# Layer A's projections as seven block products (Strassen) in a streaming encoder step

## The chip, the core and the metric

One core of a Trainium2 chip runs the whole kernel in one launch. The metric is the device time of that launch in microseconds, the median of several runs; the kernel before takes 2946.37 us (three runs, 2944.8 to 2947.03).

## What is computed

One inference step of a trunk with one layer of each kind (float32 everywhere). 640 token rows, 512 of a new stream and 8 x 16 of running ones, are 2048 wide. Layer A, the part that changes:

```python
h = rmsnorm(x, norm_a)                        # 640 x 2048
z = h @ w_in_a                                # 2048 -> 2 * 4096
u, gate = z[..., :4096], z[..., 4096:]
# 4 groups of 1024 channels; trailing mean over 2, 4, 8, 16 rows minus the row itself
y[group] = (mean(u[group], window) - u[group]) @ w_grp_a[group]     # 1024 -> 1024
x = x + (y * scale * silu(gate)) @ w_out_a    # 4096 -> 2048
```

The last 15 rows of u of every stream are outputs too. Then come one shared projection to keys and values, layer B (attention with a forgetting term over the keys of past and new rows, a gate, an output projection) and a final norm.

## The kernel before

Channels lie on the 128 partitions and the 640 tokens along the free dimension, in two halves of 320 (`HALF`). To multiply in float32r with nearly float32's accuracy, each operand is split in two: `hi` is the float32r copy (ScalarE), `lo` what is left (VectorE, `split`). A product is then three matmuls, hi·hi, hi·lo and lo·hi: `mm3` issues them for both halves, six matmuls of 320 columns for each block of 128 x 128 weights (line 93).

`gemm_pair` makes two output blocks of 128 channels: it loads weights in chunks of 2 x 128 rows by 256 columns (`wchunk`, four raw buffers, three of each split part) and accumulates over the contraction in PSUM. `u_pair` makes two blocks of u, takes the pooling differences (on VectorE, lines 333 to 360) and keeps them split; `gate_pair` makes two blocks of the gate; `y_pair` multiplies the differences of a group of 1024 channels by the group's map and the gate; `out_pairs` multiplies two such pairs (512 channels) by the rows of the output projection and adds the result to the residual `acc` in SBUF (line 413). The order is by group: four u pairs, then gates and maps by turns, with the output projection after every second map pair.

The start of layer A runs inside the first u pair: x comes in eighths of 256 channels, is turned by TensorE and split block by block while the first pair's matmuls already use the earlier blocks. The row norm is not applied to x but to the results (`R`, a factor per token).

TensorE's instructions stand in the order in which they are written (`manual_schedule`); the other engines' are ordered by a planner with a cost model. Small side work is given to TensorE's stream by generators (`work`, `tick`). All DMAs are issued on SP's queue. At the end of layer A, `after` splits the new stream, ScalarE squares it and GpSimd sums the squares (lines 466 to 473); the keys' projection (`proj`, tile `mmb`) follows at once.

## Time and profile before

| | |
|---|---|
| median of three runs | 2946.37 us |
| span of the profiled execution, first to last instruction | 2944.0 us |
| layer A, up to the first matmul of the next projection | 1610.6 us |
| TensorE busy | 2921.5 us, 99% |
| VectorE busy | 1457.7 us, 50% |
| ScalarE busy | 847.9 us, 29% |
| GpSimd busy | 34.7 us, 1% |
| moved by DMA | 293 MB, mean 100 GB/s |

The three runs are timed without a profile; the profiled execution is known by its span. A matmul's busy time overlaps that of its neighbours, so 99% says that TensorE always has one under way, not that it runs at its peak.

### The profile page before, as it was taken

What the parts mean: (1) busy time and instruction counts of PE and PEld (TensorE: products, weight loads), DVE (VectorE), ACT (ScalarE), POOL (GpSimd) and SP (SyncE); (2) the same over time, 40 slices, a digit from 0 to 9 for tenths busy, and PEclk for the clock granted to TensorE, in tenths of its full rate; (3) what the DMA queues carried; (4) which work ended last, traced back from release to release, by engine and by line L of the source; (5) the groups of instructions that cost most, each with busy time, mean ns of one, the idle gap of its engine ahead of it and who ended that gap; (6) DMA issues with size and microseconds to landing.
All of it is one profiled execution on the core that took longest, in us unless ns stands there. A gap on an engine that the chain in (4) does not pass through costs nothing.

```text
span 2944.0 us, 47606 instructions
## 1 busy us (share of the span) xinstructions
PE 2921.5 (99%) x19573; PEld 2828.4 (96%) x19573; DVE 1457.7 (50%) x2587; ACT 847.9 (29%) x1560; POOL 34.7 (1%) x73
## 2 busy tenths in 40 slices
PE   9999999999999999999999999999999999999998
PEld 9999999999999999999999899999999999999786
DVE  6423344333445333554337755655656666556434
ACT  5222222221222212222224232333333333334222
POOL 0000000000000000000003000000000000000000
PEclk9999999999999999999999999999999999999999
DMA  4222222222222222222224655455554555554822
GB/s 149 81 78 76 76 79 78 81 75 76 79 77 83 75 76 76 79 80 78 76 76 140 132 122 119 112 119 123 134 119 114 119 120 121 118 119 108 145 86 108
DMA packets 610282, 293.04 MB, mean 100 GB/s; under 512 B 281024, under 2 KB 595712, under 8 KB 609936
## 3 DMA queue, kind: packets, MB, share of 16 engines
q1 hardware_dynamic: 610064, 290.00, 38.5%
q8 instruction: 153, 2.51, 0.4%
q14 instruction: 65, 0.53, 0.1%
HBM read 261.28 MB, written 28.64 MB: 98 GB/s over the span
## 4 chain that ended last, share of the span: by engine, by line
PE 93%; DMA 2%; DVE 2%; SPq 1%; ACT 1%; issue 1%; DVEq 0%; POOL 0%; POOLq 0%; ACTq 0%
PE mm L93 35%; PE mmb L93 29%; PE mmx L93 17%; PE mmf L900 4%; PE po L832 2%; PE tb L117 1%; PE f L900 1%; PE ss L733 1%; DMA xt<-xres 1%; SPq L938 1%; DVE yn L941 0%; DMA raw<-in_w_in_b 0%; PE sp L743 0%; PE op L845 0%; PE op L844 0%
## 5 line engine op out<-in xcount | busy, mean ns | idle before, releaser
L78 DVE TENSOR_TENSOR wlo<-raw,whi 128x512 fp32r<-128x512 f32 x480 | 337.6, 704 | 793.6 <-ACT whi L75 791.4
L75 ACT ACTIVATE whi<-raw 128x512 fp32r<-128x512 f32 x480 | 302.7, 631 | 1012.2 <-PE mm L93 588.8
L93 PE MATMUL mmb<-xh,whi 128*128 128x320 f32 x2048 | 483.1, 317 | 2.6 <-DVE acc L413 2.6
L93 PE MATMUL mmb<-xh,wlo 128*128 128x320 f32 x2048 | 467.1, 309 | 0.0
L93 PE MATMUL mmb<-xl,whi 128*128 128x320 f32 x2048 | 466.9, 309 | 0.0
L93 PEld LDWEIGHTS mmb<-xh,whi 128*128 128x128 f32 x2048 | 337.1, 189 | 8.9 <-issue 6.5
L93 PEld LDWEIGHTS mmb<-xh,wlo 128*128 128x128 f32 x2048 | 342.9, 188 | 0.0
L93 PEld LDWEIGHTS mmb<-xl,whi 128*128 128x128 f32 x2048 | 342.8, 188 | 0.0
L93 PE MATMUL mm<-xh,whi 128*128 128x320 f32 x1408 | 325.8, 313 | 1.3 <-ACT xh L258 1.3
L93 PE MATMUL mm<-xl,whi 128*128 128x320 f32 x1408 | 321.7, 310 | 0.3 <-DVE xl L259 0.2
L93 PE MATMUL mm<-xh,wlo 128*128 128x320 f32 x1408 | 321.3, 309 | 0.0
L142 DVE TENSOR_TENSOR wlo<-raw,whi 128x512 fp32r<-128x512 f32 x272 | 188.3, 693 | 204.5 <-ACT whi L140 200.4
L140 ACT ACTIVATE whi<-raw 128x512 fp32r<-128x512 f32 x272 | 171.6, 632 | 377.4 <-PE mmb L93 232.1
L93 PEld LDWEIGHTS mm<-xl,whi 128*128 128x128 f32 x1408 | 235.6, 188 | 1.4 <-DVE xl L259 1.3
L93 PEld LDWEIGHTS mm<-xh,wlo 128*128 128x128 f32 x1408 | 235.8, 188 | 0.0
L93 PEld LDWEIGHTS mm<-xh,whi 128*128 128x128 f32 x1408 | 234.0, 188 | 1.8 <-ACT xh L258 1.5
L131 DVE TENSOR_TENSOR raw<-raw,cols 128x512 f32<-128x512 f32 x256 | 169.3, 676 | 4.8 <-DMA raw<-in_w_kv 2.2
L93 PE MATMUL mm<-mh,whi 128*128 128x320 f32 x688 | 157.4, 310 | 0.4 <-ACT whi L75 0.4
L93 PE MATMUL mm<-mh,wlo 128*128 128x320 f32 x688 | 156.7, 309 | 0.0
L93 PE MATMUL mm<-ml,whi 128*128 128x320 f32 x688 | 156.4, 308 | 0.0
L93 PE MATMUL mmx<-xh,whi 128*128 128x320 f32 x640 | 147.2, 311 | 0.0
L93 PE MATMUL mmx<-xh,wlo 128*128 128x320 f32 x640 | 145.8, 309 | 0.0
(306 smaller groups left out, 4187.9 us busy)
## 6 DMA issues: line engine op xcount, KB each, us to landing
raw<-in_w_in_a SPq DMA_DIRECT2D x256, 256.0 KB, 2.7
raw<-in_w_out_a SPq DMA_DIRECT2D x128, 256.0 KB, 2.8
raw<-in_w_kv SPq DMA_DIRECT2D x128, 256.0 KB, 3.0
raw<-in_w_in_b SPq DMA_DIRECT2D x128, 256.0 KB, 3.0
raw<-in_w_grp_a SPq DMA_DIRECT2D x64, 256.0 KB, 2.7
kc<-in_cache_k SPq DMA_DIRECT2D x64, 256.0 KB, 4.8
vc<-in_cache_v SPq DMA_DIRECT2D x16, 1024.0 KB, 7.6
raw<-in_w_out_b SPq DMA_DIRECT2D x64, 256.0 KB, 3.0
```

Source lines behind the costliest of these rows:

```text
L75: a = nc.scalar.activation(hi, x, AF.Copy)
L78: nc.vector.tensor_tensor(lo, x, hi.bitcast(F32), op=ALU.subtract)
L93: nc.tensor.matmul(acc_[:, s, :HALF], w, x[:, s * HALF : (s + 1) * HALF], start=f, stop=l)
L117: nc.tensor.transpose(out, x, ident[:n, :n])
L131: nc.vector.tensor_tensor(r, r, raws[n][1].unsqueeze(2).to_broadcast([P, 4, P]), op=ALU.mult)
L140: nc.scalar.activation(hi, raw, AF.Copy)
L142: nc.vector.tensor_tensor(lo, raw, hi.bitcast(F32), op=ALU.subtract)
L733: nc.tensor.matmul(sp[rows, b % 2 * PAST : (b % 2 + 1) * PAST], qs[:, rows], kct[:, b * PAST : (b + 1) * PAST], start=True, stop=True)
L832: nc.tensor.matmul(po[32 * q : 32 * q + 32, :P], pts[:, j, 32 * q : 32 * q + 32], vc[:, 4 * q + j, :], start=(j == 0), stop=False)
L900: nc.tensor.matmul(out, (ol if q == 2 else oh)[:, k, ts], wl if q == 1 else wh, start=first and q == 0, stop=last and q == 2)
L938: dma(xt[at].rearrange("p t (j r) -> p t j r", r=32), xres[n * 512 : (n + 1) * 512].rearrange("(j c) (t a r) -> a c t j r", c=32, a=4, r=3 ...
```

## The change

*Seven products for eight.* The 640 tokens and the channels are cut in two: a pair of output blocks, a pair of contraction blocks and the two halves of tokens form 2 x 2 blocks. Instead of eight block products, seven products of sums and differences are made (Winograd's form). Of the weights, `prep` makes four sums per pair on VectorE and splits seven operands; of x, `blocks_b` and `blocks_t` make the same once per pair of contraction blocks (`Side`). `product` is one of the seven: three matmuls of 320 columns. `pair8` runs a pair of u or gate blocks: four slabs of 512 contraction rows, in each all seven products, each in its own PSUM bank (bank 7 is left for small transposes); `combine` makes the four result blocks out of the seven banks. The output projection does the same over 512 rows of a half group (`out_pair`): now all 1024 rows of a group in one accumulation. The maps of the groups (`y_pair`) stay plain.

*New order.* All u and gate pairs come first (32 units); the pooling differences and the gates go to DRAM and come back for the maps; then, group by group, four map pairs and eight output pairs.

*Start.* x is loaded by rows, normalised by rows (`norm_a` included), turned, and only then split into blocks and sums; `first_unit` runs the first pair with the products that need no sums of x ahead of the others. `R` is no longer needed in layer A.

*Moved between engines.* The sliding sums of the pooling go from VectorE to GpSimd (2 to 8 adds per u pair), as do half of the sums of x, and some weight sums of the last 16 chunks. Stores of layer A go from SP's queue to GpSimd's. The residual lies in DRAM (`xacc`): `out_pair` adds to it by accumulating DMAs on GpSimd's queue, one of 640 KB and two of 160 and 320 KB for each pair of output blocks; for the last group the sum is loaded back and finished on VectorE.

*Buffers.* PSUM is one tile of eight banks, given out by hand. SBUF pools are laid anew, with waits by tile where one takes over the place of another. In layers after A only the banks, the names of buffers and the place of x (DRAM, loaded back at the start of layer B) change.

```diff
+    OPER = {"m1": (0, 0), "m6": (5, 5), "m5": (4, 3), "m7": (3, 4), "m2": (2, 2), "m3": (6, 1), "m4": (1, 6)}
...
+    def blocks_b(sd, x4):
+        sd.bh, sd.bl = (bslot(sd.j, q, [P, 3, HALF], F32R) for q in "hl")
+        nc.scalar.activation(sd.bh, x4[:, 1:4, :], AF.Copy)
+        nc.vector.tensor_tensor(sd.bl, x4[:, 1:4, :], sd.bh.bitcast(F32), op=ALU.subtract)
...
+    def blocks_t(sd, x4, t, eng=None):
+        eng = eng or nc.vector
+        eng.tensor_tensor(t[:, 0, :], x4[:, 0, :], x4[:, 1, :], op=ALU.subtract)
+        eng.tensor_tensor(t[:, 1, :], x4[:, 2, :], x4[:, 0, :], op=ALU.add)
+        eng.tensor_tensor(t[:, 2, :], x4[:, 2, :], t[:, 0, :], op=ALU.add)
+        eng.tensor_tensor(t[:, 3, :], x4[:, 3, :], t[:, 2, :], op=ALU.subtract)
+        sd.th, sd.tl = (tslot(sd.j, q, [P, 4, HALF], F32R) for q in "hl")
+        nc.scalar.activation(sd.th, t, AF.Copy)
+        nc.vector.tensor_tensor(sd.tl, t, sd.th.bitcast(F32), op=ALU.subtract)
...
+    def prep():
+        n = nprep[0]
+        raw = loaded.pop(n).rearrange("p (a b) (s n) -> p a (b s) n", a=2, n=P)
+        if loads[n][0] == "s":
+            sums = wa.tile([P, 2, 4, P], F32, tag="sums", name="sums")
+            nc.vector.tensor_tensor(sums[:, :, 0:2, :], raw[:, :, 1:3, :], raw[:, :, 0:1, :].to_broadcast([P, 2, 2, P]),
+                                    op=ALU.subtract)
+            eng = nc.gpsimd if n >= len(loads) - 16 else nc.vector
+            eng.tensor_tensor(sums[:, :, 2, :], sums[:, :, 1, :], raw[:, :, 1, :], op=ALU.add)
+            eng.tensor_tensor(sums[:, :, 3, :], raw[:, :, 3, :], sums[:, :, 2, :], op=ALU.subtract)
+            two, (wh, wl) = wbufs(n, [P, 2, 7, P])
+            todo = [(raw, slice(1, 4), slice(0, 3)), (sums, slice(0, 4), slice(3, 7))]
+        else:
+            two, (wh, wl) = wbufs(n, [P, 2, 4, P])
+            todo = [(raw, slice(0, 4), slice(0, 4))]
+        for src, a, b in todo:
+            if two is not None:
+                split(two[0][:, :, b, :], two[1][:, :, b, :], src[:, :, a, :])
+            else:
...
+    def advance():
+        d = ndone[0]
+        ahead = 3 if d < NA else 4
+        while nprep[0] < min(d + ahead, len(loads)):
+            if nload[0] <= nprep[0]:
+                fetch()
+            prep()
+        while nload[0] < min(nprep[0] + 3, len(loads)):
+            fetch()
...
+    def product(bank, m, wts, kk, sd, first, last):
+        wh, wl = wts
+        a, b = OPER[m]
+        for q, (w, x) in enumerate(((wh, sd.hi(b)), (wh, sd.lo(b)), (wl, sd.hi(b)))):
+            nc.tensor.matmul(bank[:, :HALF], w[kk][:, a, :], x, start=first and q == 0, stop=last and q == 2)
...
+    def pair8(hook=None):
+        pp = {m: banks[:, j, :] for j, m in enumerate(ORDER)}
+        for s in range(4):
+            wts = parts.pop(0)
+            advance()
+            for j, m in enumerate(ORDER):
+                for kk in range(2):
+                    product(pp[m], m, wts, kk, xs_[2 * s + kk], s + kk == 0, s == 3 and kk == 1)
+                if j == 6:
+                    done()
+                if hook is not None:
+                    hook(s, j)
+                if j in (2, 5):
+                    tick()
+        return pp
...
+        v, u, e = cvue
+        nc.scalar.activation(v, pp["m1"][:, :HALF], AF.Copy)
+        nc.vector.tensor_tensor(u, v, pp["m6"][:, :HALF], op=ALU.add)
+        nc.vector.tensor_tensor(e, u, pp["m5"][:, :HALF], op=ALU.subtract)
+        put("c22", e, "m7", ALU.subtract)
+        nc.vector.tensor_tensor(u, u, pp["m7"][:, :HALF], op=ALU.subtract)
+        put("c11", v, "m2", ALU.add)
+        put("c12", e, "m3", ALU.add)
+        put("c21", u, "m4", ALU.add)
...
+    units = [("u", 0, 0)]
+    for n in range(1, 16):
+        units += [("u", n // 4, n % 4), ("g", (n - 1) // 4, (n - 1) % 4)]
+    units += [("g", 3, 3)]
...
+    half_rows(0)
+    for q in range(4):
+        dma(gains[q], i["norm_a"][0][q * 512 : (q + 1) * 512].partition_broadcast(P))
+    half_rows(1)
+    fetch()
+    half_rows(2)
+    half_rows(3)
+    half_rows(4)
+    for _ in range(2):
+        fetch()
+    ssq = small.tile([P, TT, 4], F32, name="ssq")
...
+            nc.scalar.activation(banks[:, 7, :], rows[t][q * 512 // n][:, c : c + 512], AF.Square, accum_out=ssq[:, t, q : q + 1])
...
+            nc.vector.scalar_tensor_tensor(r, r, rs, gains[q], op0=ALU.mult, op1=ALU.mult)
...
+    for j in range(8):
+        blocks_b(xs_[j], x4s[j])
+        if j in (1, 3, 5):
+            prep()
+            for _ in range({1: 1, 3: 0, 5: 3}[j]):
+                fetch()
+    for j in range(8):
+        t = tslot({1: 4, 3: 5, 5: 6}[j], "h", [P, 4, HALF]) if j in (1, 3, 5) else x4slot()
+        blocks_t(xs_[j], x4s[j], t, nc.gpsimd if j % 2 else None)
...
+    def first_unit():
+        pp = {m: banks[:, j, :] for j, m in enumerate(ORDER)}
+        held = [parts.pop(0) for _ in range(4)]
+        for ms in (("m1", "m2", "m3"), ("m6", "m5", "m7", "m4")):
+            for s in range(4):
+                for kk in range(2):
+                    for m in ms:
+                        product(pp[m], m, held[s], kk, xs_[2 * s + kk], s + kk == 0, s == 3 and kk == 1)
+                if ms[0] == "m6":
+                    done()
+                    if s > 1:
+                        prep()
+        return pp
...
-                    nc.vector.tensor_tensor(nx[:, e0:], cur[:, e0:], cur[:, e0 - sh : UW - sh], op=ALU.add)
...
+                nc.gpsimd.tensor_tensor(nx[:, e0:], cur[:, e0:], cur[:, e0 - sh : UW - sh], op=ALU.add)
...
+            store2(dscr[4 * g + p][b * P : (b + 1) * P, :], dd)
...
+    def gate_pair(g, p, hook=None):
+        pp = pair8(hook)
+        sg = x4slot()
+        combine(pp, lambda name: [(sg[:, WHERE[name], :], slice(0, HALF))])
+        for b in range(2):
+            v = sg[:, 2 * b : 2 * b + 2, :]
+            nc.scalar.activation(v, v, AF.Silu)
+        store2(pair_rows(gscr[4 * g + p]), sg.rearrange("p (k s) n -> p k (s n)", k=2))
...
+    def d_pair(g, j, dk):
+        raw = ps_.tile([P, 2, NT], F32, tag="sg", name="draw", bufs=2)
+        dma(raw, pair_rows(dscr[4 * g + j]))
+        dk.append([tslot(j, q, [P, 2, NT], F32R) for q in "hl"])
+        split(dk[-1][0], dk[-1][1], raw)
...
+        blocks_b(y_[p], m4)
+        blocks_t(y_[p], m4, x4slot())
...
-                    a = halves(acc[:, 2 * c + b, :])
-                    nc.vector.tensor_tensor(a, pp[b][:, :, :HALF], a, op=ALU.add)
...
+    def out_pair(g, c, x1=None):
+        pp = {m: bank()[:, :HALF] for m in ORDER}
+        wts = [parts.pop(0), parts.pop(0)]
+        advance()
+        def go(m, s):
+            for kk in range(2):
+                product(pp[m], m, wts[s], kk, y_[2 * s + kk], s + kk == 0, s + kk == 2)
+        for m, s in [(m, s) for s in range(2) for m in ORDER[:4]] if c == 0 else [(m, s) for m in ORDER[:4] for s in range(2)]:
+            go(m, s)
+        u = misc.tile([P, HALF], F32, tag="cu", name="cu")
+        o4 = m4slot() if c % 2 or x1 is not None else x4slot()
+        nc.scalar.activation(o4[:, 3, :], pp["m1"], AF.Copy)
+        nc.vector.tensor_tensor(u, o4[:, 3, :], pp["m6"], op=ALU.add)
+        nc.vector.tensor_tensor(o4[:, 2, :], u, pp["m5"], op=ALU.subtract)
+        nc.vector.tensor_tensor(o4[:, 0, :], o4[:, 2, :], pp["m7"], op=ALU.subtract)
+        nc.vector.tensor_tensor(o4[:, 1, :], u, pp["m7"], op=ALU.subtract)
+        nc.gpsimd.dma_start(pair_rows(xacc[c]), o4.rearrange("p (k s) n -> p k (s n)", k=2), accum_op=ALU.add)
+        if x1 is not None:
+            for k in range(2):
+                dma(x1[k], xacc[c][k * P : (k + 1) * P, :])
+        for m, s in (("m2", 0), ("m3", 0), ("m2", 1), ("m3", 1), ("m4", 0), ("m4", 1)):
+            go(m, s)
+            if m == "m4":
+                done()
+                if s == 0:
+                    advance()
+        if x1 is None:
+            o3 = bslot(2, "hl"[c % 2], [P, 3, HALF])
+            for m, j in (("m2", 2), ("m3", 1), ("m4", 0)):
+                nc.scalar.activation(o3[:, j, :], pp[m], AF.Copy)
+            nc.gpsimd.dma_start(xacc[c][:P, HALF:], o3[:, 0, :], accum_op=ALU.add)
+            nc.gpsimd.dma_start(xacc[c][P:, :], o3[:, 1:, :].rearrange("p s n -> p (s n)"), accum_op=ALU.add)
+        else:
+            for m, j in (("m2", 3), ("m3", 2), ("m4", 1)):
+                a = halves(x1[j // 2])[:, j % 2, :]
+                nc.vector.tensor_tensor(a, a, pp[m], op=ALU.add)
+    first = first_unit()
+    start.close()
+    su = ExitStack()
+    pu = pool(su, "pu")
+    for n, (kind, g, p) in enumerate(units):
+        if n == 1:
...
+    late = []
+    for g in range(4):
+        for p in range(4):
+            y_pair(g, p, gates.pop(0), dk)
+            if p < 2:
+                gates.append(load_gate(g, p + 2))
+        nd = []
+        for c in range(8):
+            if g < 3:
+                out_pair(g, c)
+                if c < 4:
+                    d_pair(g + 1, c, nd)
+                elif c > 5:
+                    gates.append(load_gate(g + 1, c - 6))
+            else:
+                if c % 4 < 3:
+                    x1 = ps_.tile([P, 2, NT], F32, tag="sg", name="x1", bufs=2) if c % 4 < 2 else \
+                        x4slot().rearrange("p (k s) n -> p k (s n)", k=2)
+                    x1 = [x1[:, 0, :], x1[:, 1, :]]
+                else:
+                    x1 = [bslot(3, q, [P, NT]) for q in "hl"]
+                out_pair(g, c, x1)
+                for k, x in zip((2 * c, 2 * c + 1), x1):
+                    store2(xres[k * P : (k + 1) * P, :], x)
+                    squares(k, x)
+                    if k < 8:
+                        split_x(k, x)
+                    else:
+                        late.append((k, x))
+        dk = nd
+    store2(sqd, sqs[0])
+    for k, x in late:
+        split_x(k, x)
+    sa.close()
```


## Rows read from the trace of the kernel before

**Rows 1.** The page, its first part (busy time of each engine, share of the span, instructions) and three lines of its second (the span in 40 equal slices; busy tenths of TensorE and VectorE, then the clock granted to TensorE in tenths of full speed).
```profile
PE 2921.5 (99%) x19573; PEld 2828.4 (96%) x19573; DVE 1457.7 (50%) x2587; ACT 847.9 (29%) x1560; POOL 34.7 (1%) x73
...
PE   9999999999999999999999999999999999999998
...
DVE  6423344333445333554337755655656666556434
...
PEclk9999999999999999999999999999999999999999
```

**Rows 2.** The chain of work that ended last, merged, in order of time: start, length in us, engine, operation, tile, line, count. A piece is only matmuls that followed one another.
```profile
104.92 0.21 PE tb L117 x2
...
179.81 28.16 PE mm L93 x192
...
758.92 24.64 PE mm L93 x168
...
1610.60 8.53 PE mmb L93 x46
...
2879.30 33.73 PE mmf L900 x144
```

**Rows 3.** Windows: stretch and length in us; for each engine busy us and instructions; then granted clock, mean busy share of the DMA engines, GB/s.
```profile
0.00:52.00 52.00, 47.72 (x307) 44.67 (x308) 35.09 (x86) 37.25 (x75) 0.81 (x7) 0.97 0.56 178
...
1610.00:1720.00 110.00, 106.83 (x762) 101.02 (x763) 73.45 (x142) 31.48 (x56) 8.40 (x22) 0.98 0.61 130
...
0.00:25.00 25.00, 21.73 (x125) 19.97 (x126) 14.21 (x42) 15.75 (x30) 0.70 (x6) 0.93 0.86 280
...
100.00:1500.00 1400.00, 1399.61 (x9559) 1398.98 (x9558) 572.96 (x895) 334.96 (x599) 3.01 (x27) 1.00 0.27 78
```

**Rows 4.** Groups of instructions by line and form, VectorE: out<-in, partitions x elements, count | busy us, mean ns of one | idle time before them, and what ended it.
```profile
L78 DVE TENSOR_TENSOR wlo<-raw,whi 128x512 fp32r<-128x512 f32 x480 | 337.6, 704 | 793.6 <-ACT whi L75 791.4
...
L78 DVE TENSOR_TENSOR dl<-dd,dh 128x640 fp32r<-128x640 f32 x32 | 26.3, 822 | 6.2 <-ACT dh L75 5.6
...
L348 DVE TENSOR_TENSOR sw<-ub 128x774 f32<-128x774 f32 x32 | 30.8, 963 | 3.3
...
L517 DVE STREAM_TRANSPOSE kn<-kt 128x640 f32<-128x640 f32 x16 | 13.3, 833 | 0.0
...
L353 DVE SCALAR_TENSOR_TENSOR dd<-sw,ub 128x511 f32<-128x511 f32 x8 | 5.5, 683 | 0.0
...
L356 DVE SCALAR_TENSOR_TENSOR dd<-sw,ub 128x128 f32<-128x128 f32 x32 | 9.1, 283 | 0.0
...
L754 DVE RECIPROCAL rw<-rw 128x1 f32<-128x1 f32 x64 | 10.0, 156 | 2.1 <-ACT pr L753 1.4
...
L337 DVE TENSOR_TENSOR ub<-mm,R 128x320 f32<-128x320 f32 x22 | 10.8, 489 | 11.5 <-PE mm L93 9.1 <-ACT R L284 2.2
...
L338 DVE TENSOR_TENSOR ub<-mm,R 128x192 f32<-128x192 f32 x22 | 7.6, 347 | 0.0
...
L340 DVE TENSOR_TENSOR ub<-mm,R 128x128 f32<-128x128 f32 x22 | 6.2, 280 | 0.0
...
L259 DVE SCALAR_TENSOR_TENSOR xl<-tb,cols,xh 128x512 fp32r<-128x512 f32 x8 | 6.0, 749 | 4.5 <-ACT xh L258 4.5
...
L246 DVE TENSOR_TENSOR xg<-tp,cols 128x256 f32<-128x256 f32 x8 | 3.4, 419 | 0.2 <-PE tp L117 0.2
```

**Rows 5.** Instructions in order of time where GpSimd adds up squares beside VectorE, just before and in the hand-over to layer B: start us, length us, engine, line, operation, tile, form. The form with `sq` is GpSimd's, the last row is VectorE's subtraction without GpSimd beside it.
```profile
1566.32 1.58 POOL L473 TENSOR_TENSOR sq<-sq,sqk 128x640 f32<-128x640 f32 x1 [3.09 <-ACT sqk L472]
...
1566.39 0.82 DVE L413 TENSOR_TENSOR acc<-mm,acc 128x640 f32<-128x640 f32 x1
...
1597.85 1.73 POOL L473 TENSOR_TENSOR sq<-sq,sqk 128x640 f32<-128x640 f32 x1 [0.85 <-ACT sqk L472]
...
1598.07 2.19 DVE L78 TENSOR_TENSOR xl<-acc,xh 128x640 fp32r<-128x640 f32 x1
...
1602.40 0.83 DVE L78 TENSOR_TENSOR xl<-acc,xh 128x640 fp32r<-128x640 f32 x1 [0.81 <-ACT xh L75]
```

**Rows 6.** As rows 4, ScalarE.
```profile
L75 ACT ACTIVATE whi<-raw 128x512 fp32r<-128x512 f32 x480 | 302.7, 631 | 1012.2 <-PE mm L93 588.8 <-PE mmx L93 295.9 <-PE f L900 64.1
...
L269 ACT ACTIVATE junk<-xq 128x1024 f32<-128x1024 f32 x10 | 10.6, 1062 | 0.1
```

**Rows 7.** DMA issues: out<-in, queue, operation, count, size, median us from issue to landing. All of them stand on SP's queue; a store is one whose left side is an output or a DRAM buffer (xres, sv).
```profile
raw<-in_w_out_a SPq DMA_DIRECT2D x128, 256.0 KB, 2.8
...
raw<-in_w_kv SPq DMA_DIRECT2D x128, 256.0 KB, 3.0
...
vc<-in_cache_v SPq DMA_DIRECT2D x16, 1024.0 KB, 7.6
...
xres<-acc SPq DMA_DIRECT2D x4, 1280.0 KB, 5.2
...
sv<-vx SPq DMA_DIRECT2D x64, 80.0 KB, 2.1
```

More of the change, by code (lines that the diff above doesn't have):

```diff
@@ L487, in norm_stream @@
+    with tc.tile_pool(name="pn", bufs=1, reuse_waits="tile") as pn:
+        sq = pn.tile([P, NT], F32, name="sq2")
+        dma(sq, sqd)
+        def norm_stream():
+            for _ in range(3):
+                yield
+            ones = make_ones(pn, "ones")
+            v = pn.tile([P, NT], F32, name="v2")
             for s in range(2):
@@ L596, in forget @@
             yield
[L597 removed]
+            pl = mmbank()
             for k in range(KT):
```

696 lines of the change are left out of this document (367 added, 329 removed).

## The prediction

> **What bounds the kernel now.** The page's first two parts come first [rows 1]: TensorE is busy 99% of the span, VectorE 50%, ScalarE 29%, and the granted clock is at full speed (2.4 GHz) in all 40 slices. So the question is how many matmuls there are and how fast they come. The chain of waits gives the pace [rows 2]: 192 matmuls of 320 columns in 28.16 us and 168 in 24.64 us, 146.7 ns each, one behind the other. The busy shares alone would hide that: a matmul shows 309 ns since neighbours overlap. The windows then say where there is any slack [rows 3]: between 100 and 1500 us TensorE misses 0.4 us in 1400; it loses time only in the first 52 us and around the hand-over to layer B at 1610. Nothing but fewer columns can shorten layer A, and any new wait is paid in full.
>
> Layer A ends where the first matmul of the next projection starts, at 1610.60 us [rows 2]. Its 10,752 matmuls (32 input pairs of 192, 16 map pairs of 96, 64 output pairs of 48) take 10,752 x 0.1467 = 1577.0 us. Of the 33.6 us left, 68 small transposes for the pooling rows take 0.106 us each [rows 2], 7.2 us, and the start 26.4 us.
>
> **The change part by part.**
>
> *Fewer matmuls.* Seven products instead of eight blocks: an input pair takes 4 x 7 x 2 x 3 = 168 matmuls, an output pair (now over 512 rows at once) 84 instead of two times 48; the maps stay. 32 x 168 + 1536 + 32 x 84 = 9600, which is 1152 fewer, or **169.0 us**. The pace should hold: they have the same 320 columns, and every matmul of before has its own weight load already (19573 of each, [rows 1]). New are six matmuls in a row into one bank; the nearest row, the last projection with runs of three into one bank, takes 234 ns for 512 columns [rows 2], which is the same 0.457 ns a column, so I price that at nothing. Layer A is then 1408.0 + 7.2 us plus what follows.
>
> *The start.* Before, the first matmuls stood between the transposes, block by block. Now the rows are normalised first, and the products need all blocks and sums of x. I add up VectorE, from forms of the old start and their neighbours [rows 4]. A two-input op costs 0.69 to 0.70 us for 512 elements, 0.82 for 640, 0.96 for 774, so about 1.05 ns an element and 0.15 fixed: 0.42 for 256, 0.49 for 320, 1.16 for 960, 1.22 for 1024, 1.49 for 1280. Per row tile four scalings (0.75), a short root (about 1.1 over seven ops of 0.1 to 0.2) and two evictions (0.42) make 4.95, five tiles 24.7. The four weight slabs, each with 0.69 + 2 x 0.42 for sums and 0.96 + 1.22 for the low parts, 3.71 us: 14.8. Low parts of the plain blocks 8 x 1.16 = 9.3, sums of the even sides 4 x 4 x 0.49 = 7.8, low parts of the sums 8 x 1.49 = 11.9. Together 68.5 us. GpSimd makes the sums of the odd sides, 16 ops of half of 1.58 us [rows 5] = 12.6 us, and these hold VectorE up (below). From about 9 us on (the first megabyte takes 3.7 us at the 280 GB/s of the first 25 us [rows 3] and about one to issue; four squares follow) the last sums are there at 78 to 90 us, and one slab of four products (24 matmuls, 3.5 us) is left: the first pair ends near 87 us instead of after its own 24.6. I take **62 us** for the start against 26.4; 45 if VectorE does all weight slabs while it waits for x, 80 if the sequence also waits for ScalarE.
>
> *VectorE and GpSimd in the input stage.* A u pair and a gate pair take TensorE 2 x 24.64 + 0.4 = 49.7 us. VectorE does eight slabs (29.7), the gate's seven combining ops (3.4), the u pair's (3.7, two of them cut in pieces of 192 and 128), the differences (2.4) and a turn of x (0.84): 40.1 us, [rows 4]. That alone fits, and the combining hides: its products end one after the other 0.88 us apart, the next pair writes the same bank 6.2 us later. But the sliding sums move to GpSimd: 2(g+1) per u pair, 774 elements each. The trace has GpSimd adding only 640 elements, in 1.58 us [rows 5], so 1.9 us each: 3.8, 7.6, 11.5 and 15.3 us per pair for g = 0 to 3. [rows 5] show what this does to VectorE: the low part at 1598.07 takes 2.19 instead of 0.82 us, 1.37 more, with 1.51 of GpSimd's add left; an add with one input in PSUM, at 1566.39, takes its usual 0.82 under such an add. So VectorE's two-input SBUF ops and GpSimd's adds queue behind one another: 43.9, 47.7, 51.6 and 55.4 us against 49.7. Four pairs each of the last two exceed by 4 x (1.9 + 5.7) = 30 us. Weights are prepared two slabs (12.3 us) ahead, and up to 7.1 us of combining can run under GpSimd: I take **20 us**; none if all of it does, 40 if the waits bunch up.
>
> *Maps and output.* An output pair gives VectorE two slabs (7.4), four evictions (2.0) and in half of them a split (1.5) against 84 x 0.1467 = 12.3 us: it fits. What is late is the last map pair of each group: its two evictions (1.0), four sums (2.0), ScalarE's high parts (about 1.28 for 1280 elements, from 1.06 for 1024 in [rows 6]) and the low parts (1.5) end 5.8 us after its last matmul, while the next output pair can do four products of its first half and one more, 30 matmuls or 4.4 us. That is 1.4 us, and 5.1 with one weight slab ahead in VectorE's queue: **20 us** for four groups; bounds 4 and 36.
>
> *Hand-overs and DMAs.* Into the maps the differences come back from DRAM into two buffers, four loads and splits within half a pair: **3 us** (0 to 8). Into layer B eight splits of x (8 x 0.82 = 6.6) lie beside the first 48 matmuls (7.0), but the first weights need buffers that the last products still read: load 2.7 to 3.0 [rows 7] plus three ops of 0.6 to 0.7, some of it covered: **5 us** (0 to 10). GpSimd's queue takes over the stores and the accumulating writes; no row shows such a write. The nearest are stores of 80 KB in 2.1 us and 1280 KB in 5.2 [rows 7]. An output pair issues one of 640 KB, and two more that must wait for it to land, which would take some 7 to 10 us of its 12.3. In the last group the loads of the sums stand on SP's queue behind the accumulation, ahead of weights that are fetched three deep: **5 us** in all (0 to 30).
>
> *Sum.* 1415.2 + 62 + 20 + 20 + 3 + 5 + 5 = 1530 us instead of 1610.6: 80.4 us less. Everything from 1610.6 on keeps its work, 1333.4 us, so the span is 2863.6. The profiled span, 2944.0, lies 2.4 below the median of the three runs, 2946.37; with the same 2.4 the time is **2866 us**.
>
> **Rivals.**
> (a) *Nearly all is kept.* Slabs are prepared in VectorE's idle time of the start (47 us), GpSimd's adds fall under the combining (3), the turn to the output costs its 1.4 us (6), the rest 5: 1415.2 + 61 = 1476, so 2812 us. For it: VectorE at 40 of 49.7 us per pair. Against it: [rows 5].
> (b) *VectorE becomes the bound of the input stage.* If ops on views of three dimensions cost more than these rows, and the waits behind GpSimd are longer, 3 us more for each u and gate pair together (16 x 3 = 48), 2914 us. For it: the excess of the last two groups; against it: 50% today.
> (c) *Slower: the accumulating writes pace the output stage.* In an output pair the second and third write wait in GpSimd's queue until the first has landed, and the next pair's first write is queued behind them. The cycle decides from the point where it exceeds 12.3 us, and undoes the rest of the gain at 12.3 + 80.4/32 = 14.8. With landings as slow as the slowest large transfer of the old kernel, 7.6 us for the first [rows 7], the same for the two others before their buffers turn, and 1 us of issue, 16.2: 32 x 3.9 = 125 us more, 2991 us. Against it: stores of twice the size land in 5.2.
> The Trainium skill (DMA: Bandwidth & Descriptors, "Anatomy of one DMA — SWDGE (gpsimd) path") puts a DMA issued by GpSimd at 2.0 us plus its bytes over 436 GB/s, an estimate of 3.5 us for 640 KB; by that the cycle stays under 12.3 us and (c) falls away. No run here shows it. The same notes (SBUF — State Buffer, the warning on the "DVE blocks DMA" trap) say that VectorE can keep GpSimd from writing descriptors; by that the issue would be long and (c) likelier. No row of before has a DMA on GpSimd's queue, so the chance of (c) stays as the stores make it.
> (d) *The pace drops*, since products change bank and operands more often: 13.3 ns more per matmul (as much as 146.7 already lies over 320 columns at 2.4 GHz) would cost 128 us on 9600 and leave 2994 us. Against it: the row of runs into one bank.
>
> **How the numbers follow.** Forecast 2866 us, own range 2830 to 2900, chance 0.58; (a) 0.16; (b) 0.14; (c) 0.09; (d) 0.03. All but (c) and (d) are faster by far more than 0.2% (6 us, about what a measurement of this kernel can tell from no change); with all upper bounds together (startup 80, 40, 36, 8, 10, 30) the time is 2955, so I leave 0.03 for no change and 0.12 for slower: faster 0.85. The range that leaves out no more than 2 in 10 reaches down to (a) and over (b): 2815 to 2940.
>
> **What would show it.** 5376 + 1536 + 2688 matmuls in layer A and 24.6 us per undisturbed pair prove the first step; 27 us or more without TensorE waiting proves (d). The end of the first pair near 87 us tests the start. In the input stage TensorE should be gapless for g = 0 and 1 and lose some 2 and 6 us per two pairs later, with VectorE's low parts above 1.2 us whenever GpSimd adds; gaps from the first group on mean (b), none mean (a). Waits of TensorE at each turn from maps to output test the 5 us. Releasers that name the accumulating writes, with output pairs above 12.3 us, mean (c). If the start ends past 100 us or the output pairs exceed 14 us, the forecast is wrong.

## The result: 16 us faster, where 80 were forecast

The changed kernel takes 2930.56 us (median of four runs, 2929.89 to 2931.91) against 2946.41 for the kernel before beside it: 0.9944 of its time, 95% interval 0.993 to 0.9958. The forecast was 2866, its range 2815 to 2940. The time lies in that range, above the narrower one of 2830 to 2900, and the sign is right, but four fifths of the gain are missing.

The page of the changed kernel, parts 1 and 2, answers to [rows 1]:

```profile
span 2929.3 us, 46530 instructions
PE 2794.5 (95%) x18410; PEld 2691.4 (92%) x18410; DVE 1935.2 (66%) x3350; ACT 1027.0 (35%) x1720; POOL 390.5 (13%) x426
...
PE   5899999999999999999986999999999999999998
...
PEclk9799999999999999999997999999999999999999
```

TensorE has 1163 instructions fewer and is busy 95% instead of 99% of a span that is 14.7 us shorter. The slices name two places: the first two and, at about half of the span, the end of layer A. Both also show a lower granted clock. What the slices are too coarse for is a third place between them. TensorE's waits, first from the end of the first pair to the first map (line, releaser, sum in us, times, longest), then from the first map to layer B:

```profile
PE banks L110 <- ACT po L485: 21.2, 9, 3.4
...
PE banks L701 <- ACT whi L730: 22.7, 1, 22.7
PE banks L246 <- DVE x L605: 14.1, 4, 5.9
PE banks L246 <- DVE tl L173: 8.4, 4, 2.3
PE banks L246 <- DVE bl L605: 4.8, 1, 4.8
```

By stages: the first pair of output blocks ends near 104 us (forecast 87). The first map starts at 910.3; the other 31 pairs and the small transposes are 771 us, so 35 us are lost in this input stage (forecast 20). The last group's output, from 1445.8 to 1577.4, takes 131.6 us, where eight pairs of 12.3 and a turn of 5 from maps to output make 104: 28 us too much (forecast 5). The gap to layer B is 22.7 us (forecast 5). With 4.2 us less from there on and nothing seen of the 3 us into the maps, 17 + 15 + 23 + 17.7 - 4.2 - 3 = 65.5 us: the whole difference between the forecast gain of 80.4 and the 14.7 of the spans.

Waits are not all of it. In the input stage they add up to 23.6 of the 35 us, in the last group to 21.6 of the 33 that it takes beyond its matmuls. Much of the rest is matmuls that come further apart at a lower granted clock (the last section shows two of them). It is 0.97 from 600 to 750 us, and in the last group it falls to 0.88 (stretch, length, busy time and instructions of TensorE, weight loads, VectorE, ScalarE and GpSimd, granted clock, DMA share, GB/s):

```profile
1520.00:1560.00 40.00, 29.72 (x176) 29.20 (x177) 25.10 (x38) 15.30 (x22) 20.52 (x22) 0.88 0.58 158
```

The input stage can be read in 20 us. VectorE, ScalarE, GpSimd and one line of TensorE in the last group there (start, duration, engine, line, operation, and in brackets the idle time before it and its releaser):

```profile
751.61 1.70 DVE L213 TENSOR_TENSOR sums<-raw,sums 128x256 f32<-128x256 f32 x1
...
753.10 5.83 POOL L463 TENSOR_TENSOR sw<-sw 128x772 f32<-128x772 f32 x3
...
758.97 0.18 DVE L466 TENSOR_TENSOR dd<-sw,inv 128x15 f32<-128x15 f32 x1 [3.25 <-POOL sw L463]
...
761.86 0.42 DVE L213 TENSOR_TENSOR sums<-raw,sums 128x256 f32<-128x256 f32 x1
...
762.31 1.06 ACT L86 ACTIVATE wh<-sums 128x1024 fp32r<-128x1024 f32 x1 [5.66 <-DVE sums L213]
763.27 0.26 ACT L485 ACTIVATE po<-banks 120x128 f32<-120x128 f32 x1
...
763.59 0.32 PE L110 MATMUL banks<-ident,us 128*120 128x128 f32 x1 [2.34 <-ACT po L485]
```

Read from below: TensorE turns (transposes) the second block of pooling rows into bank 7 and waits 2.34 us for ScalarE's copy of the first. That copy stood in ScalarE's order behind a weight's high part, which had waited 5.66 us for VectorE's weight sums. These were late because VectorE, in its own order, had waited 3.25 us for GpSimd's sliding sums, and because some of its ops on SBUF take longer while GpSimd adds (1.70 us instead of 0.42 for the same 256 elements). The weights themselves were still in time; a side job of 0.26 us was not.

### The profile page after: what moved, and what is told of

Its sections match the earlier page's. It is cut to its first block, busy times and chain, and to the rows that moved or that the text cites. A ratio compares the mean times of both kernels' runs of the same rounds, so it can differ in the third digit from the quotient of the medians.

```text
span 2929.3 us, 46530 instructions
## 1 busy us (share of the span) xinstructions
PE 2794.5 (95%) x18410; PEld 2691.4 (92%) x18410; DVE 1935.2 (66%) x3350; ACT 1027.0 (35%) x1720; POOL 390.5 (13%) x426
## 3 DMA queue, kind: packets, MB, share of 16 engines
q0 software_dynamic: 25168, 66.78, 10.4%
## 4 chain that ended last, share of the span: by engine, by line
PE 42%; DMA 4%; DVE 1%; SPq 1%; POOL 1%; issue 1%; ACT 0%; DVEq 0%; POOLq 0%; ACTq 0%
PE banks L701 30%; PE banks L1205 5%; PE banks L1133 2%; DMA xacc<-m 2%; PE banks L1034 1%; DMA xt<-xres 1%; PE banks L110 1%; SPq L1243 1%; DMA x<-xacc 1%; POOL bh L640 1%; PE banks L1044 0%; PE banks L1045 0%; PE banks L1046 0%; DVE yn L1246 0%; PE banks L1146 0%
## 5 line engine op out<-in xcount | busy, mean ns | idle before, releaser
L246 PE MATMUL banks<-th,wh 128*128 128x320 f32 x1408 | 447.9, 318 | 12.6 <-ACT th L172 12.2
L246 PE MATMUL banks<-tl,wh 128*128 128x320 f32 x1408 | 442.9, 315 | 17.7 <-DVE tl L173 17.7
L246 PE MATMUL banks<-th,wl 128*128 128x320 f32 x1408 | 441.3, 313 | 0.0
L701 PE MATMUL banks<-th,whi 128*128 128x320 f32 x2048 | 399.6, 317 | 22.7 <-ACT whi L730 22.7
L701 PE MATMUL banks<-tl,whi 128*128 128x320 f32 x2048 | 384.0, 309 | 0.0
L246 PE MATMUL banks<-bh,wh 128*128 128x320 f32 x1056 | 332.8, 315 | 14.8 <-DVE x L605 9.8
L246 PE MATMUL banks<-bl,wh 128*128 128x320 f32 x1056 | 331.8, 314 | 3.1 <-DVE bl L163 3.1
L246 PE MATMUL banks<-bh,wl 128*128 128x320 f32 x1056 | 331.6, 314 | 0.6 <-DVE wl L89 0.6
L732 DVE TENSOR_TENSOR wlo<-raw,whi 128x512 fp32r<-128x512 f32 x272 | 186.3, 686 | 212.9 <-ACT whi L730 209.9
L701 PEld LDWEIGHTS banks<-tl,whi 128*128 128x128 f32 x2048 | 321.9, 188 | 0.0
L246 PEld LDWEIGHTS banks<-tl,wh 128*128 128x128 f32 x1408 | 270.4, 192 | 20.9 <-DVE tl L173 20.9
L246 PEld LDWEIGHTS banks<-th,wh 128*128 128x128 f32 x1408 | 270.5, 192 | 17.2 <-ACT th L172 15.2
```

Of the source, the lines that this page charges most:

```text
L246: nc.tensor.matmul(bank[:, :HALF], w[kk][:, a, :], x, start=first and q == 0, stop=last and q == 2)
L701: nc.tensor.matmul(acc_[:, s, :HALF], w, x[:, s * HALF : (s + 1) * HALF], start=f, stop=l)
L732: nc.vector.tensor_tensor(lo, raw, hi.bitcast(F32), op=ALU.subtract)
```

## Experiments

Ratios are to the kernel before, in runs beside it; the changed kernel is 0.9944. Each interval reaches 0.0014 to 0.0017 to either side, 4 to 5 us, so differences of a few us between two runs are not clear of noise.

| run | edit | median us | ratio |
|---|---|---|---|
| e1_rows_on_sp | pooling rows stored from SP | 2934.69 | 0.9955 |
| e2_sums_on_dve | sliding sums on VectorE | 2900.35 | 0.9839 |
| e3_second_o4 | two buffers for four results | 2932.87 | 0.9943 |
| e4_squares_late | squares loaded behind weights | 2929.79 | 0.9937 |
| e5_rows_apart | own columns in bank 7 | 2928.65 | 0.9929 |
| e6_x1_ahead | no accumulating write at the end | 2909.27 | 0.9870 |
| e7_x_sums_on_dve | sums of x on VectorE | 2918.26 | 0.9897 |
| e8_squares_off_pool | squares, stores off GpSimd | 2924.56 | 0.9922 |
| e9_rows_later | second turn of rows later | 2921.05 | 0.9914 |
| e10_raw_free | e4, small tile zeroed on VectorE | 2932.68 | 0.9950 |
| e11_both_ways_out | e3 and e8 together | 2928.30 | 0.9922 |
| c1_four_parts | e2 + e4 + e6 + e7 | 2866.54 | 0.9725 |
| c3_five_parts | c1 + zeroing of e10 | 2866.49 | 0.9729 |
| c4_wr_behind | c1, small load behind the weights | 2863.51 | 0.9717 |
| c5_last_sums | c4, last weight sums on VectorE | 2854.61 | 0.9688 |

**The input stage.** The first theory put the late copies on GpSimd's queue of stores.

```diff
-            store2(o["pool_sample"][0]...
+            store(o["pool_sample"][0]...
```

> The nine stores per group that carry the pooling rows go back from GpSimd's queue to SP's. Theory (the pooling rows hold PSUM bank 7: their one SBUF buffer is freed only when a store gets past the sliding sums in GpSimd's queue): TensorE's waits for ScalarE's copy of the rows, 20.8 us in the input stage, go; first matmul of the maps at about 890 instead of 910 us, time 2908 to 2915. Rival (VectorE, slowed by GpSimd's adds, delivers the weights late): no wait changes, time within 4 us of 2930.6.

Nothing moved: TensorE's waits for the copy are 21.6 us instead of 21.2, so that theory fell. This trace showed what stands ahead of the copy:

```profile
655.62 1.06 ACT L86 ACTIVATE wh<-sums 128x1024 fp32r<-128x1024 f32 x1 [6.60 <-DVE sums L213]
...
656.59 0.26 ACT L485 ACTIVATE po<-banks 120x128 f32<-120x128 f32 x1
...
656.90 0.32 PE L110 MATMUL banks<-ident,us 128*120 128x128 f32 x1 [3.28 <-ACT po L485]
```

The copy runs when ScalarE gets past the weight's high part, store or no store. The direct test takes the sums back from GpSimd.

```diff
-                nc.gpsimd.tensor_tensor(nx[:, e0:], cur[:, e0:], ...
+                nc.vector.tensor_tensor(nx[:, e0:], cur[:, e0:], ...
```

> The sliding sums go back to VectorE; nothing else changes. An add of 774 elements is about 0.96 us there, so 1.9 to 7.7 us more per u pair, and VectorE's own ops lose the waits behind GpSimd. Theory (queue of GpSimd holds bank 7): input stage loses its 20.8 us of waits for the pooling rows; VectorE at 40 + 7.7 of 49.7 us still fits, time 2900 to 2912, low parts of the weights in group 3 back at about 1.22 instead of 1.31 us. Rival (VectorE is the bound of the input stage): waits move to weights, loss in groups 2 and 3 as now or larger, time 2925 to 2950.

The first map starts at 878.6 instead of 910.3 us, and from 150 us on no wait is left in the stage. The time is at the lower end of the theory's range, but the mechanism that the theory names, GpSimd's queue, had fallen with e1; what the run shows is that GpSimd's adds are behind the loss. The same stretch, 455 to 870 us, in the changed kernel and then in this run (columns as above):

```profile
455.00:870.00 415.00, 394.64 (x2649) 390.65 (x2647) 328.82 (x505) 141.00 (x218) 123.95 (x119) 0.99 0.41 121
```

```profile
455.00:870.00 415.00, 415.00 (x2841) 414.79 (x2840) 351.79 (x592) 159.26 (x236) 38.29 (x79) 1.00 0.45 134
```

VectorE is busier and nobody waits for it. What sharing had cost it is in its own rows between 660 and 910 us, the changed kernel first (count, then busy us, mean ns):

```profile
L89 DVE TENSOR_TENSOR wl<-sums,wh 128x1024 fp32r<-128x1024 f32 x36 | 47.8, 1328 | 15.2 <-ACT wh L86 15.2
...
L209 DVE TENSOR_TENSOR sums<-raw 128x512 f32<-128x512 f32 x35 | 28.7, 821 | 0.8
L213 DVE TENSOR_TENSOR sums<-raw,sums 128x256 f32<-128x256 f32 x35 | 26.0, 742 | 0.8
L212 DVE TENSOR_TENSOR sums<-sums,raw 128x256 f32<-128x256 f32 x35 | 19.4, 554 | 0.9
```

```profile
L89 DVE TENSOR_TENSOR wl<-sums,wh 128x1024 fp32r<-128x1024 f32 x34 | 41.5, 1221 | 13.1 <-ACT wh L86 13.0
...
L209 DVE TENSOR_TENSOR sums<-raw 128x512 f32<-128x512 f32 x34 | 23.4, 689 | 0.5
L213 DVE TENSOR_TENSOR sums<-raw,sums 128x256 f32<-128x256 f32 x34 | 14.4, 424 | 0.6
L212 DVE TENSOR_TENSOR sums<-sums,raw 128x256 f32<-128x256 f32 x34 | 14.4, 422 | 0.4
L463 DVE TENSOR_TENSOR sw<-ub 128x774 f32<-128x774 f32 x8 | 7.7, 962 | 0.1
```

Under GpSimd's adds these four kinds cost VectorE 36 x 0.107 + 35 x (0.132 + 0.318 + 0.132) = 24 us more, and it waited another 11.5 us for GpSimd's results. Making all 32 sliding sums itself costs 30.6 us there (four rows like the last). The help was worth less than nothing.

Two runs tried to give the copy room instead. In e5 the two turns use different columns of bank 7.

> The two turns of pooling rows of a u pair get columns of their own in PSUM bank 7 (256 to 383 and 384 to 511) instead of the same first 128; every engine keeps its work. Theory now (GpSimd's adds lengthen VectorE's weight sums; ScalarE's high part waits for these, and the copy of the pooling rows stands behind it in ScalarE's order, so TensorE waits at bank 7 although the weights would still be in time): TensorE's 21.2 us of waits for the copy go and do not come back elsewhere, time 2902 to 2912, VectorE's long sums unchanged. Rival (VectorE's lost time has to be paid in any case): the waits move to the weights' parts, time 2922 to 2931.

It told nothing of the two theories: the waits for the copy stayed (19.9 us). Perhaps the program still waits for the bank as a whole; no run shows it. In e9 the second turn comes three steps later.

```diff
             yield
+            if b and g > 1:
+                yield
+                yield
+                yield
             tq = tbank()
```

> In groups 2 and 3 TensorE turns the second block of pooling rows three ticks (some 10 us of matmuls) after the first instead of one tick (3.5 us); nothing moves between engines. Theory (VectorE's weight sums, lengthened by GpSimd's adds, hold ScalarE's order up, and the copy of the rows in it; the weights themselves are in time): TensorE's waits for the copy fall from 21 to under 6 us with nothing in their place, time 2905 to 2914. Rival (VectorE's time is short in groups 2 and 3 in any case): the same 15 to 20 us come back as waits for weight parts or banks, time 2924 to 2931.

Neither theory got it: half of the 21 us came back as other waits, the first map starts at 900.3. From 455 us on TensorE's waits read (line 489 is line 485 of the changed kernel)

```profile
PE banks L246 <- ACT cv L284: 7.2, 3, 2.6
PE banks L110 <- ACT po L489: 4.8, 2, 3.6
```

So the copy was only the first in ScalarE's order to be missed. The next one, the copy of product m1 that frees its bank, is held up by the same late weight sums: ScalarE makes it right behind a weight's high part that had waited for them, all three times.

**The start.**

```diff
-        blocks_t(xs_[j], x4s[j], t, nc.gpsimd if j % 2 else None)
+        blocks_t(xs_[j], x4s[j], t)
```

> At the start all sums of x are made on VectorE, 16 ops of 320 elements moved from GpSimd. Theory (GpSimd's adds and VectorE's hold one another up, so sharing gains nothing): first pair ends 8 to 13 us earlier than 104, time 2917 to 2923. Rival (one buffer for the sums of the even sides, or ScalarE between sums and low parts, sets the pace): first pair within 3 us of 104 or later, time 2928 to 2936.

As the theory had it: the first map comes 12.9 us earlier (897.4), the time is 0.5% less. Between 50 and 75 us VectorE was busy 18.70 us and GpSimd 11.35; without GpSimd's help VectorE fills the stretch:

```profile
50.00:75.00 25.00, 18.78 (x107) 16.95 (x105) 24.93 (x39) 12.36 (x13) 0.00 (x0) 0.93 0.07 22
```

In the changed kernel the two had held each other up:

```profile
70.27 2.02 DVE L173 TENSOR_TENSOR tl<-x,th 128x1280 fp32r<-128x1280 f32 x1
70.90 2.11 POOL L169 TENSOR_TENSOR th<-tl,th 128x320 f32<-128x320 f32 x1
73.09 0.87 POOL L170 TENSOR_TENSOR th<-tl,th 128x320 f32<-128x320 f32 x1
74.00 1.27 ACT L172 ACTIVATE th<-th 128x1280 fp32r<-128x1280 f32 x1 [3.76 <-POOL th L170]
```

The low part takes 2.02 instead of 1.49 us, GpSimd's next add 2.11 instead of 0.87, and ScalarE waits for the last of these.

**The last group.** GpSimd's queue in one period of the changed kernel:

```profile
1495.49 1.23 POOL L586 DMA_DIRECT2D xacc<-m  x1
...
1506.03 0.60 POOL L673 DMA_DIRECT2D xres<-x  x1 [3.91 <-DVE x L605]
1506.65 1.57 POOL L640 TENSOR_TENSOR bh<-bh,bl 128x640 f32<-128x640 f32 x1
...
1509.08 1.57 POOL L640 TENSOR_TENSOR bh<-bh,bl 128x640 f32<-128x640 f32 x1 [0.35 <-ACT bl L638]
...
1513.30 1.25 POOL L586 DMA_DIRECT2D xacc<-m  x1
```

The accumulating write of a pair is issued at 1495.49. SP issues the load back at 1501.97, when the write has landed. VectorE adds m2 to m4, x is stored and squared, and only behind that comes the next write, 17.8 us after the first where a pair has 12.3 us of matmuls; the eight writes of the group are 16.6 us apart on average. There were three candidates for what closes this loop: the single buffer of the four results, GpSimd's order, and the PSUM banks.

> In the last group the four results of an output pair go by turns into two buffers instead of one, and x1 gets other places for it; no transfer is added or taken away. Theory (one buffer, held until the accumulating write of 6 to 10 us has landed, paces the last group): ScalarE's 25 us of waits for that write shrink to under 6, the last eight output pairs take about 108 instead of 131.7 us, time 2906 to 2914. Rival (the chain write, landing, load back, add, banks free paces it, buffer or not): the wait moves to the load of x1 and to the banks, gain 0 to 8 us, time 2922 to 2931.

```diff
-        o4 = m4slot() if c % 2 or x1 is not None else x4slot()
+        o4 = m4slot() if (c % 2 if x1 is None else c not in (1, 3, 5)) else x4slot()
```

(x1 got other buffers for this.) The wait for the buffer, in the changed kernel

```profile
ACT m L581 <- DMA xacc<-m: 25.2, 7, 8.1
```

went and the time did not: the group takes 131.0 us.

> In the last group the sums of squares go from GpSimd to VectorE, and the stores of x from GpSimd's queue to SP's; the accumulating writes and the loads back stay. Theory (the loop of 17 us a pair passes through GpSimd's order, where the next write stands behind this pair's store and sums of squares): the write no longer waits for the load back, pairs of 13 to 15 us, last product at 1550 to 1562, time 2903 to 2916. Rival (the landing of the accumulating write, its load back and the banks held meanwhile pace the pairs by themselves): 16.5 us and more a pair, time 2925 to 2932.

```diff
-            nc.gpsimd.tensor_tensor(sqs[0], sqs[0], s, op=ALU.add)
+            nc.vector.tensor_tensor(sqs[0], sqs[0], s, op=ALU.add)
...
-                    store2(xres[k * P : (k + 1) * P, :], x)
+                    store(xres[k * P : (k + 1) * P, :], x)
```

Some 6 us, at the edge of noise (the group takes 128.0 us, the gap behind it 20.5), and the single buffer still shows (ScalarE waits 20.9 us for the write). So the two might have hidden one another:

> The two edits of the last group that gave nothing and 6 us alone, together: two buffers for the four results, and the sums of squares and the stores of x taken from GpSimd. Theory (two loops of the same length stand side by side, one through the single buffer and one through GpSimd's order, and each edit alone leaves the other): the accumulating write of a pair now waits for neither, output pairs of 13 to 14.5 us, last product near 1552 to 1560, time 2903 to 2914. Rival (the time of the write, its load back, the adds and the banks held meanwhile is itself longer than a pair): pairs stay at 15.5 us and more, time 2920 to 2927.

Only in part. With both ways out open, ScalarE's wait for the write is left once, the group takes 125.0 us, and writes are issued 15.2 us apart on average (1499.79 to 1575.82, five periods; 16.1 in the last five of the changed kernel). That is above the 13 to 14.5 of the theory, the time is no better than with e8 alone, and TensorE waits as before:

```profile
PE banks L246 <- DVE x L605: 14.3, 4, 6.2
```

That leaves the banks, and TensorE's row of waits names the adds that free them: a pair takes seven of the eight, and m2 to m4 keep theirs until the write has landed and x1 is back and added to. The next run takes the write and the load back out of the pairs of the last group, so that it removes the loop and not one of its three parts:

```diff
+            for k in range(2):
+                nc.vector.tensor_tensor(x1[k], x1[k], o4[:, 2 * k : 2 * k + 2, :].rearrange("p s n -> p (s n)"), op=ALU.add)
...
+                if c < 7:
+                    load_x1(c + 1)
```

> In the last group the residual is loaded one pair ahead and the four results are added to it on VectorE, two adds of 640 elements a pair; the eight accumulating writes of 640 KB and the loads behind them go. Theory (a loop of 17 us a pair: accumulating write 6.4, load back 3.3, adds, store and sum of squares on GpSimd, and the next write queued behind these): output pairs of the last group fall to 12.5 to 13.5 us, last product near 1551 instead of 1577, the gap before layer B to 12 to 18 us, time 2893 to 2903. Rival (the late group is bound by VectorE and GpSimd work that stays: splits, squares, sums of weights): pairs stay above 15 us, time 2915 to 2931.

The wait on x is gone, the group takes 114.4 us (1447.3 to 1561.7) instead of 131.6, and the gap behind it 17.9 instead of 22.7 us: together 22 us, where 21 were measured. The time lies between the ranges of theory and rival: the pairs are still (114.4 - 5) / 8 = 13.7 us, a little above what the theory gave, and small waits for weight parts have come in:

```profile
PE banks L246 <- DVE wl L89: 3.7, 4, 1.4
PE banks L246 <- ACT wh L86: 3.7, 3, 2.2
```

**The hand-over to layer B.** SP's queue in the changed kernel; the last product ends at 1577.4 us:

```profile
1582.65 0.32 SPq L589 DMA_DIRECT2D bh<-xacc  x1
...
1589.80 0.38 SPq L1157 DMA_DIRECT2D wr<-in_w_kv  x1
...
1594.85 0.34 SPq L780 DMA_DIRECT2D sq<-sqd  x1
1595.23 2.08 SPq L716 DMA_DIRECT2D raw<-in_w_kv  x4
```

The first weights (`raw`) stand behind a load back, behind a small tile `wr` whose zeroing waits in GpSimd's order, and behind the sum of squares.

> The load of the sums of squares is issued behind the first weight loads of layer B instead of ahead of them. Theory (the first weights stand on SP's queue behind a load that waits for the last squares, their sum on GpSimd and its store): TensorE's 22.7 us gap at the hand-over shrinks by 8 to 12 us, time 2918 to 2923. Rival (the weights wait for buffers that the last products and splits still hold): gap within 2 us of 22.7, time 2929 to 2931.

> At the hand-over to layer B the load of the sums of squares is issued behind the first weight loads, and the zeroing of one small tile (whose load stands ahead of the weights on SP's queue) goes from GpSimd to VectorE. Theory (SP's queue: the weights are held by loads that wait for GpSimd, which is still adding squares): first weight load issued near 1586 instead of 1595 us, gap of TensorE 13 to 16 instead of 22.7 us, time 2920 to 2925. Rival (the weights' buffers are still held by the last splits on VectorE until about 1592): gap 19 to 22 us, time 2927 to 2931.

Neither theory got its gain, and both rivals, the buffers, seemed borne out. Moving the squares (`dma(sq, sqd)` behind `prime()`) gave nothing measurable. In e10 the gap was 23.6 us, since the zeroing, once on VectorE, stood behind VectorE's splits: `wr` was issued at 1590.38 of a run that was ahead by 2.6 us, so later than before. A wait had changed its name. c4 makes the zeros from a value that exists only later, so that `wr` falls behind the weights:

```diff
-            nc.gpsimd.memset(wr, 0.0)
+            nc.vector.tensor_scalar(wr.rearrange("p a b -> p (a b)"), R[:, :512], 0.0, None, op0=ALU.mult)
```

> The kernel with four edits, and the small tile's zeros are made from the token factors of the norm, which are there only after the first projection: its load no longer stands ahead of the weights on SP's queue. Theory (SP's order holds the first weights, the buffers are free): first weight load right behind the last product (issue near 1516 instead of 1525 us), gap at the hand-over 8 to 11 instead of 17.2 us, time 2857 to 2861. Rival (the weights' buffers lie where the last x and its splits still are): the load waits as long for VectorE, gap 15 to 18, time 2864 to 2868.

Now the gap is 10.4 us instead of 17.2, with the weights issued 3 us after the last product:

```profile
1517.59 0.33 SPq L1031 DMA_DIRECT2D kc<-in_cache_k  x1
...
1520.29 2.59 SPq L729 DMA_DIRECT2D raw<-in_w_kv  x4
```

SP's order held them, then, not the buffers. Of the 7 us only 3 reach the time, within the noise, since the last product came 3 us later in this run (1517.7 against 1514.4). All of it is in the last group: the same code there takes 113.4 us in c1, 114.4 in e6, 115.4 in c3 and 116.5 here; why it varies was not looked for. The rest of the gap is VectorE, which splits x until 1526.6 before it scales the first weights.

**Together.** 

> Sliding sums and sums of x on VectorE, x1 loaded ahead and added there, sums of squares loaded behind the weights: four edits in different stages. Theory (each stage lost its time to its own chain, so the gains of the single edits, 30, 12, 21 and 1 us, add up): 2930.6 - 64 = 2866, time 2860 to 2874. Rival (they share something, such as the clock granted after a stall or VectorE's time, and overlap): time 2878 to 2895.

2866.54 us: the gains of single stages add up (30 + 12 + 21 + 1 = 64 us). TensorE misses nothing in this run from 100 to 880 us:

```profile
100.00:600.00 500.00, 500.00 (x3421) 499.46 (x3421) 404.64 (x697) 187.24 (x286) 47.50 (x101) 1.00 0.44 130
600.00:880.00 280.00, 280.00 (x1917) 279.86 (x1916) 233.56 (x387) 107.00 (x157) 27.12 (x55) 1.00 0.48 143
```

> The same four edits and the small tile zeroed on VectorE. With the load back gone from the hand-over the first theory of the queue expects 3 to 6 us less than the kernel with four edits (2856 to 2870); the rival (weights' buffers held by the splits) expects the same time as with four edits within 2 us.

The same time as c1, as e10 would have it. c5, with the edits of c4, asks about GpSimd once more, in the last group:

```diff
-            eng = nc.gpsimd if n >= len(loads) - 16 else nc.vector
+            eng = nc.vector
```

> As the kernel before it in this call, and the weight sums of the last eight output pairs go from GpSimd to VectorE (32 ops of 256 elements, 13 us more work for VectorE in about 110 us, where it is busy 80 to 87%). Theory (GpSimd's adds cost VectorE more than it would lose by doing them itself): last product 3 to 8 us earlier, time 2850 to 2857. Rival (VectorE is the bound of the last group and has no room): last product 5 to 10 us later, time 2862 to 2872.

The last product ends at 1508.8 instead of 1517.7 us and the time is 2854.61, although VectorE had been busy for more than four fifths of that group. Now it is busy 39.7 of the 40 us from 1440 to 1480, and the group takes 105.8 us, close to its 104. This version beats both kernels: 0.9688 of the time before, interval 0.9673 to 0.9702.

## Why the prediction was right in kind and wrong in size

**Fewer matmuls: right.** Layer A has the 9600 matmuls forecast, and undisturbed stretches run at 500 / 3421 = 0.146 us per matmul, small transposes included. The pace did not drop, so rival (d) is out, and 169 us were really removed. All that is missing was put back by new waits and the lower clock behind them.

**The start: 62 us taken, 79 measured.** The step that failed is the sum "VectorE 68.5 us, GpSimd beside it". It gave GpSimd the odd sides' sums for nothing but a remark that they hold VectorE up. e7 shows that they cost 12.9 us more than they spared: with all sums on VectorE the pair ends at 91 us. The remaining 4 us have two causes that the rows show and no run took apart: ScalarE's high part stands between sums and low part, and behind the later stalls TensorE ran at half clock (below).

**The input stage: 20 us taken, 35 measured.** The cause was named, that VectorE's SBUF ops and GpSimd's adds queue behind one another, and its size was of the right order (24 us of longer ops in the last group's stretch, where 30 were forecast for two groups). The step that failed is what followed from it. I compared VectorE's sum with TensorE's time per pair and let two slabs of stock absorb the rest. But orders are passed on: VectorE waits in its order for GpSimd's results (11.5 us), ScalarE in its order for VectorE's sums, and TensorE for a copy behind these. Lower granted clock behind the waits came on top. The Trainium skill (SBUF — State Buffer, "SBUF: two separate sides") says that the two engines share a port pair, an exclusive lock for a whole instruction, which also holds between a VectorE op with two SBUF inputs and a GpSimd op that reads SBUF. The trace agrees: under GpSimd's add an op of 0.42 us took 1.70. The Trainium skill (Perfetto Trace Analysis, "Optimizing Scalar/DVE Operations") warns that moving work between these two engines might not help. Here each of three such moves, undone, gave time back (30, 12 and 9 us).

**Turns from maps to output: right.** 20 us for four were forecast. From the first map to the last group's first output pair, with three turns, 535.5 us pass for 521 us of matmuls: 4.8 us per turn.

**The last group: 5 us taken (0 to 30), some 28 measured.** The sentence on "the loads of the sums on SP's queue behind the accumulation" saw the chain, and priced it as one of many small things. That term is the step that failed. It is a loop, run eight times: write, landing, load back, adds, banks. Rival (c) had the mechanism and the condition (cycle above 12.3 us). Its place was wrong: in the first three groups TensorE waits for no landing, and they run at their pace. By the Trainium skill (DMA: Bandwidth & Descriptors, "Anatomy of one DMA — SWDGE (gpsimd) path") 640 KB take an estimated 3.5 us. That is too low for an accumulating write here, 6.3 to 9.9 us; plain stores of 640 KB on the same queue took 3.5 to 6.1. The Trainium skill's warning (SBUF — State Buffer, the "DVE blocks DMA" trap) that VectorE's ops in a 2-port mode keep GpSimd from writing descriptors did not show here: issues on that queue took 0.5 to 1.3 us.

**The hand-over to layer B: 5 us taken, 22.7 measured.** I counted the weights' load and three ops, about 5 us if they start with the last product. They started 18 us later: behind the load back of the last pair (5 us), then behind `wr` and the squares, which wait in other engines' orders. The step that failed is that the forecast looked at buffers, not at what stands ahead of the load in SP's queue.

**Rivals (a) and (b).** (a) fell, though c1 and c5 show that most of it was there to be had. (b) had one condition right, longer waits behind GpSimd (11.5 us in the last group's stretch). VectorE as the bound of the input stage fell with e2: with 30 us more work in the stretch it still keeps TensorE fed.

That c1 measures 2866.54, the forecast to half a microsecond, is luck. Its first pair ends 5 us later than forecast, its last group takes 5 us more than the sum had for it and its hand-over 12 more; against that, its input stage loses 4 us where 20, and 3 into the maps, were taken. What c1 does show is the base of the sum: the matmuls of layer A at their old pace, and the same 1333 us from layer B on.

## What to carry to other kernels

Work moved to GpSimd is not free for VectorE: price it by the longer VectorE ops under it and by the wait for its result in VectorE's order, against what VectorE would take itself (0.96 us here for an add that cost GpSimd 1.5 to 2.3). For each small job in TensorE's stream ask what stands ahead of its helper in that helper's order; an average of busy time has no answer to that. A write to DRAM that is read back within a pipeline step is a loop: add up issue, landing, load and what holds banks meanwhile, and compare it with the step, before counting buffers.

## What the runs showed of the hardware that I had not expected

An accumulating write of 640 KB holds GpSimd's queue for 1.2 us and lands after 6.3 to 9.9 us (median 7.2, about 6.5 in the last group). A plain store of the same size on that queue holds it for 0.74 us and lands after 3.5 to 6.1 (median 5.7).

Between the waits of the start TensorE's clock fell to the lower level, 1.2 GHz. From 75 to 100 us, where TensorE was busy 14.27 of the 25 us, neighbouring matmuls of the changed kernel are 0.27 us apart instead of 0.147:

```profile
88.08 0.47 PE L246 MATMUL banks<-th,wl 128*128 128x320 f32 x1
88.35 0.47 PE L246 MATMUL banks<-th,wh 128*128 128x320 f32 x1
```

The granted clock of 75 to 100 us is 0.64 and of 100 to 125 us 0.81, so a stall can cost more than its own length; the sum of the start had priced the last 24 matmuls at full speed. Not every stall does: behind the 2.34 us at 763 us the matmuls come 0.15 us apart again at once.
